# A gated trunk layer on one core: a written order for the products of neighbouring up pairs, row loads tied to the weights in the down stage, and the half sums of eight weight pairs made in the first half's output stage

## The chip, the cores and the metric

The kernel runs on one core of one Trainium2 chip. The metric is the device time of one execution in microseconds (us); lower is better. Engines are named as in the profile: PE is TensorE's matmuls, PEld its weight loads, DVE is VectorE, ACT is ScalarE, POOL is GpSimd, SP is SyncE, which here only issues transfers. "SPq", "POOLq" and "ACTq" are the transfer queues of the engines that issue them.

## What is computed

One layer, 1024 positions by 1024 channels, in float32: a layer norm, a wide projection, a convolution branch and a state space branch, their gated sum times w_o, a layer norm, a gated MLP with a causal convolution of three taps, a layer norm.

```
h = layer_norm(x)
u = h @ w_in                      # glu | z | x,B,C | dt | gate_a | gate_b
y_a = conformer(u_glu)            # causal convolution of 31 taps
y_b = ssd(z, xBC, dt)
h = layer_norm(a*h + (sigmoid(gate_a)*y_a + sigmoid(gate_b)*y_b) @ w_o)
up = causal_conv3(h @ w_ffn_up)   # 1024 -> 2 * 2816
gate, val = split(up)
h = layer_norm(a*h + (silu(gate) * val) @ w_ffn_down)
```

## The kernel before, in words

Every product of two matrices is made of three matmuls (`mm3`, L163): each operand is split into a rounded high part (ACT copies it into the type that PE takes, L154, L740) and the rest (DVE subtracts, L155, L741), and high*high, high*low and low*high are added in one PSUM bank. So each weight tile costs one load from HBM (SP), one cast on ACT and one subtraction on DVE before PE can use it. PSUM has two pools of four banks, `acc` and `sm`.

The positions are worked in two halves of 512. For each half come `ln_in`, `mixers` (four groups of columns, convolutions and the state space part) and `combine`. For the first half `out_proj` (L665) then multiplies by w_o in two passes q of 512 channels. A pass holds all four `acc` banks, one for each block of 128 positions; after it DVE adds the residual rows, `r = ALPHA*r + acc` (L687), which frees the banks for the next pass. The rows `r` (four tiles, pool `rows0`, L118) are loaded from `h_scr` by SP (L670). The four rows of x of the second half are normalised meanwhile by `ln_in(1)`, and `first_columns` (L348) of the second half's mixers follows on PE.

In the second half `ffn_blocks` works w_o and forms sums of blocks of the normalised rows, with which the up product (1024 x 1024 by 1024 x 5632) is made by seven products of half blocks in place of eight. A pair j of two weight tiles, with blocks a11, a12 | a21, a22, needs four half sums on DVE (L848 to L851) and the splits w24, w10 and w3; from pair 8 on also the split `ue` of the raw tile. LEAD = 8: for the first eight pairs two of the seven products (of raw tile 2j with b11 and b21) are made ahead by `up_first` (L815) while the last rows are still being normalised, and wait in HBM (`first_scr`). `up_rest` (L857) makes the other five products of a pair (of pairs 8 to 21 all seven), evicts the banks on the way (L868, L871, L878, L880, L883, L884, L886, L888), runs the three taps on DVE and ACT, gates, and stores. The sums of one bank go on after a copy was taken: PE may add to `ps` again only when ACT has read it.

`down` multiplies by w_ffn_down in seven products p of 11 steps k in the same way. Its residual rows (8 tiles of 1024 numbers, tile `rows`) are loaded by POOL in `load_rows` (L950), called at step 4 of the products 0, 1, 2 and 4.

What sets the order: the program is written in this sequence, and a scheduler (`schedule_with_timeline_sim`, L1237) reorders the instructions of each engine by data, buffers and priorities; `tc.high_priority(offset=n)` moves a block ahead. On the chip each engine then goes through its own list in order, and a waiting instruction holds all behind it, transfers included. Pools are memory regions stacked one above the other: a pool that opens after another has closed takes the same addresses, and its tiles wait for the last use of what lay there. `comb0`, `rows0`, `mixers1`, `trans` and `up` all begin at the same address.

```
with pool("rows0") as pl:
    rs = [pl.tile([P, D], F32, name=f"r0_{t}") for t in range(4)]
    out_proj(pl, rs, 0, mixT)
```

Of the kernel before, what the change touches and what calls it, by code (L numbers as in the profile page):

```python
# [16 lines left out]
P = 128  # L17
# [39 lines left out]
def kernel(  # L57
# [79 lines left out]
    h_scr = [dram.tile([HALF, D], F32, name=f"h_scr{i}") for i in range(2)]  # L137
    h1_scr = dram.tile([T, D], F32, name="h1_scr")
    first_scr = [dram.tile([2, P, HALF], F32, name=f"first_scr{j}") for j in range(LEAD)]
    NK = NF // 2  # L140
    b11_scr = [dram.tile([P, HALF], F32, name=f"b11_scr{k}") for k in range(NK)]
    b2_scr, t32_scr, t41_scr = (
# [669 lines left out]
            "t4": lambda i: b2[0][:, i, 4:8, :],  # L812
        }

    def up_first(upp, fp, bl, j):  # L815
# [12 lines left out]
        for q, block in enumerate(("b11", "b21")):  # L828
            product(ps, lambda i: w[i][:, q * HALF : (q + 1) * HALF], bl[block], q == 0)
            f = fp.tile([P, HALF], F32, tag="first", bufs=2, name=f"first{q}_{j}")  # L830
            A.copy(f, ps)
            A.dma_start(first_scr[j][1 - q], f)

    def up_weights(upp, j):


        with tc.high_priority(offset=2000):
            r1 = wst.tile([P, D], F32, tag="st", name=f"ra{j}")
            SY.dma_start(r1, wup[2 * j])
            if j:  # L840
                r2 = upp.tile([P, D], F32, tag="raw", bufs=3, name=f"rb{j}")
            else:
                r2 = wst.tile([P, D], F32, tag="st", name=f"rb{j}")
            SY.dma_start(r2, wup[2 * j + 1])
            a11, a12, a21, a22 = r1[:, :HALF], r1[:, HALF:], r2[:, :HALF], r2[:, HALF:]
            ue = None if j < LEAD else split_pair(wsp, r1, f"ue{j}")
            s3 = upp.tile([P, HALF], F32, tag="s3", name=f"s3_{j}")
            V.tensor_tensor(out=s3, in0=a11, in1=a21, op=ALU.add)  # L848
            V.tensor_tensor(out=a21, in0=a21, in1=a22, op=ALU.add)
            V.tensor_tensor(out=a11, in0=a21, in1=a11, op=ALU.add)  # L850
            V.tensor_tensor(out=a12, in0=a12, in1=a11, op=ALU.add)  # L851
# [5 lines left out]
    def up_rest(upp, us, bl, j, before, ws):  # L857

        ue, w24, w10, w3 = ws or up_weights(upp, j)
        ug, uv = us[2 * j % 3], us[(2 * j + 1) % 3]
        s = upp.tile([P, HALF], F32, tag="s", bufs=2, name=f"s{j}")
        early, late = slice(2, 2 + HALF), slice(2 + HALF, 2 + T)
        ps, pz = bank(1), bank(0)
        if ue:
            product(ps, lambda i: ue[:, i, :HALF], bl["b11"], True)
            A.copy(s, ps)  # L868
            py = bank(1)
            product(py, lambda i: ue[:, i, HALF:], bl["b21"], True)  # L870
            V.tensor_tensor(out=ug[:, early], in0=s, in1=py, op=ALU.add)  # L871
        else:
            with tc.high_priority(offset=2500):
                SY.dma_start(
                    ug[:, 2 : 2 + T].rearrange("p (q n) -> p q n", q=2),
                    first_scr[j].rearrange("q p n -> p q n"),
                )
            A.copy(ps, ug[:, late])  # L878
        product(ps, lambda i: w24[:, i, :HALF], bl["t2"], False)
        A.copy(s, ps)  # L880
        product(pz, lambda i: w3[:, i], bl["t3"], True)
        product(ps, lambda i: w10[:, i, :HALF], bl["t1"], False)
        A.copy(uv[:, late], ps)  # L883
        V.tensor_tensor(out=uv[:, late], in0=pz, in1=uv[:, late], op=ALU.subtract)  # L884
        product(pz, lambda i: w10[:, i, HALF:], bl["t4"], False)
        V.tensor_tensor(out=uv[:, early], in0=pz, in1=s, op=ALU.subtract)  # L886
        product(ps, lambda i: w24[:, i, HALF:], bl["b22"], False)
        A.copy(ug[:, late], ps)  # L888
        os = []
        j = j // 2 + j % 2 * NK  # L890
        for jj, u in ((j, ug), (NF + j, uv)):
# [25 lines left out]
        early, late = slice(0, HALF), slice(HALF, T)  # L917
        if j < NK:
            G.dma_start(b11_scr[j], ov[:, early])
            return ov  # L920
        SY.dma_start(b2_scr[j - NK], ov)
        a, b, t = before, ov, og
        V.tensor_tensor(out=t[:, early], in0=a[:, late], in1=b[:, late], op=ALU.subtract)
        V.tensor_tensor(out=a[:, late], in0=a[:, early], in1=a[:, late], op=ALU.subtract)
        V.tensor_tensor(out=t[:, late], in0=t[:, early], in1=a[:, early], op=ALU.subtract)
# [4 lines left out]
    def down(upp, dp):  # L930
# [16 lines left out]
        E, L = slice(0, HALF), slice(HALF, D)  # L947
        gb = []

        def load_rows(p):  # L950
# [140 lines left out]
        for p, (banks, first, then) in enumerate(products):  # L1091
            end = NK - LAST if p == 6 else NK
            for k in range(end):
                w = load(p, k)
                for t in range(4):
                    block(banks[t], w, t, first, k)
                if k == 4 and p in (0, 1, 2, 4):
                    load_rows(p)
# [35 lines left out]
    with pool("firsts", side="right") as fp:  # L1134
        for j in range(LEAD):
            if j == LEAD - 1:
                ws = up_weights(upp, 0)
            up_first(upp, fp, bl, j)
    before = None
    for j in range(NF):  # L1140
        before, ws = up_rest(upp, us, bl, j, before, ws), None
    ffn_stack.close()
    dp = ctx.enter_context(pool("down", side="right"))
    down(upp, dp)
# [99 lines left out]
```

## Time and profile before

| | us |
|---|---|
| median of 3 runs | 2024.91 |
| lowest and highest | 2024.34, 2026.39 |
| the profiled execution | 2030.47 |
| its span, first to last instruction | 2028.8 |
| PE busy | 1975.8 (97%) |
| DVE busy | 1695.8 (84%) |
| ACT busy | 1017.4 (50%) |
| POOL busy | 175.5 (9%) |

Times in the views count from the start of the span. Stages on PE in this execution: first half until 658, x's transposes and the second w_o pass to 686, `first_columns` 686 to 704, the second half's mixers from there, the up pairs from about 1400 to 1797, the down stage from there to the end. In a row of a group, the number behind "x" is the count, then come busy time in us, the mean in ns, and behind the second bar the idle time of the engine just before these instructions with what ended it. "PEclk" is the granted TensorE clock as a share of full speed.

### The profile page before, as it was taken

How to read it: one execution, taken by the hardware profiler on the slowest of the kernel's cores; microseconds unless marked ns; L12 is line 12 of the kernel's file. 1: busy time of each engine (PE TensorE's matmuls, PEld its weight loads, DVE VectorE, ACT ScalarE, POOL GpSimd, SP SyncE). 2: the span in 40 equal slices, each digit the busy share in tenths (PEclk: the TensorE clock that was granted, in tenths of full speed). 3: DMA queues.
4: the chain of work that ended last, by engine and by line, in shares of the span. 5: the costliest groups of instructions: out<-in, count | busy, mean ns of one | idle time of the engine just before them, and what ended most of it. 6: DMA issues, size and time to landing. Idle time of an engine off the chain costs nothing.

```text
span 2028.8 us, 24542 instructions
## 1 busy us (share of the span) xinstructions
PE 1975.8 (97%) x9164; PEld 1622.4 (80%) x9164; DVE 1695.8 (84%) x2261; ACT 1017.4 (50%) x1480; POOL 175.5 (9%) x140
## 2 busy tenths in 40 slices
PE   7999999999999999999999999999999999999998
PEld 6888888888788888888888888887777777777886
DVE  7599999989766869999998976596897777788768
ACT  4465654556453356665454645364554534443432
POOL 2010101001400000110100130010000000030000
PEclk9999999999999999999999999999999999999999
DMA  6222233333546522222323354565342222367563
GB/s 219 94 64 93 79 103 104 99 104 101 175 131 220 194 94 73 91 81 77 126 89 104 109 167 139 186 234 202 135 172 83 99 107 102 101 252 252 176 225 109
DMA packets 96903, 272.20 MB, mean 134 GB/s; under 512 B 11088, under 2 KB 11088, under 8 KB 96784
## 3 DMA queue, kind: packets, MB, share of 16 engines
q1 hardware_dynamic: 88864, 246.78, 36.8%
q0 software_dynamic: 5616, 19.66, 2.5%
q10 hardware_dynamic: 2304, 4.20, 0.6%
q8 instruction: 72, 1.18, 0.2%
q14 instruction: 47, 0.39, 0.1%
HBM read 221.05 MB, written 49.55 MB: 133 GB/s over the span
## 4 chain that ended last, share of the span: by engine, by line
PE 72%; DVE 19%; DMA 4%; issue 3%; ACT 2%; SPq 0%; DVEq 0%; ACTq 0%
PE acc L166 19%; PE acc L167 19%; PE acc L168 19%; DVE c L420 6%; PE sm L168 3%; PE sm L166 3%; PE sm L167 3%; PE sm L534 2%; PE acc L357 1%; DVE xbc L375 1%; DVE fo L898 1%; DMA dr<-b_scr 1%; PE sm L515 1%; PE sm L192 1%; PE sm L523 1%
## 5 line engine op out<-in xcount | busy, mean ns | idle before, releaser
L420 DVE SCALAR_TENSOR_TENSOR c<-v,pc,c 128x512 f32<-128x512 f32 x480 | 374.9, 804 | 6.3 <-ACT c L409 4.9
L478 POOL TENSOR_TENSOR au<-seg_mv,head_of 128x1024 fp32r<-128x1024 f32 x32 | 76.4, 2388 | 959.1 <-PE sm L487 728.8
L166 PE MATMUL acc<-hT,w_c 128*128 128x512 f32 x352 | 141.0, 401 | 0.0
L167 PE MATMUL acc<-hT,w_c 128*128 128x512 f32 x352 | 140.6, 399 | 0.0
L168 PE MATMUL acc<-hT,w_c 128*128 128x512 f32 x352 | 138.4, 393 | 0.0
L898 DVE SCALAR_TENSOR_TENSOR fo<-u,pc,fo 128x1024 f32<-128x1024 f32 x88 | 111.4, 1279 | 7.5 <-ACT fo L894 7.4
L375 DVE SCALAR_TENSOR_TENSOR xbc<-u,pc,xbc 128x512 f32<-128x512 f32 x144 | 109.9, 775 | 0.7 <-ACT xbc L373 0.5
L166 PE MATMUL acc<-h1s,w_s 128*128 128x512 f32 x264 | 103.6, 396 | 6.3 <-ACT s L880 3.7
L167 PE MATMUL acc<-h1s,w_s 128*128 128x512 f32 x264 | 102.9, 390 | 0.0
L168 PE MATMUL acc<-h1s,w_s 128*128 128x512 f32 x264 | 102.8, 391 | 0.0
L167 PE MATMUL acc<-w_z,hT 128*128 128x512 f32 x256 | 100.8, 394 | 0.0
L166 PE MATMUL acc<-w_z,hT 128*128 128x512 f32 x256 | 100.8, 401 | 0.0
L168 PE MATMUL acc<-w_z,hT 128*128 128x512 f32 x256 | 100.7, 396 | 0.0
L1032 ACT CAST w_dn<-dr 128x1024 fp32r<-128x1024 f32 (+1 forms) x73 | 60.9, 842 | 75.8 <-DVE dr L962 37.8
L154 ACT CAST w_c<-st_c 128x1024 fp32r<-128x1024 f32 x50 | 52.5, 1051 | 88.9 <-PE acc L168 68.2
L1033 DVE TENSOR_TENSOR w_dn<-dr,w_dn 128x1024 fp32r<-128x1024 f32 (+1 forms) x73 | 69.8, 963 | 15.3 <-ACT w_dn L1032 15.1
L167 PEld LDWEIGHTS acc<-hT,w_c 128*128 128x128 f32 x352 | 66.1, 188 | 16.9 <-issue 3.9
L168 PEld LDWEIGHTS acc<-hT,w_c 128*128 128x128 f32 x352 | 66.1, 188 | 16.2 <-issue 2.6
L166 PEld LDWEIGHTS acc<-hT,w_c 128*128 128x128 f32 x352 | 66.1, 188 | 15.9 <-issue 2.6
L166 PE MATMUL acc<-h1b,w_ue 128*128 128x512 f32 x168 | 67.3, 400 | 11.1 <-ACT w_ue L740 8.4
L155 DVE TENSOR_TENSOR w_c<-st_c,w_c 128x1024 fp32r<-128x1024 f32 x47 | 60.5, 1288 | 20.2 <-ACT w_c L154 20.2
L740 ACT CAST w_s<-rb 128x1024 fp32r<-128x1024 f32 x22 | 23.0, 1048 | 98.4 <-PE sm L168 63.8
(353 smaller groups left out, 5755.4 us busy)
## 6 DMA issues: line engine op xcount, KB each, us to landing
st_c<-wcol SPq DMA_DIRECT2D x50, 512.0 KB, 3.5
st_z<-wz SPq DMA_DIRECT2D x32, 512.0 KB, 3.5
st_wo<-wo SPq DMA_DIRECT2D x24, 512.0 KB, 4.0
ra<-wup SPq DMA_DIRECT2D x22, 512.0 KB, 3.6
rb<-wup SPq DMA_DIRECT2D x22, 512.0 KB, 3.4
t_scr<-fo POOLq DMA_DIRECT2D x22, 512.0 KB, 3.8
dr<-t_scr SPq DMA_DIRECT2D x44, 256.0 KB, 3.5
dr<-wdown SPq DMA_DIRECT2D x38, 256.0 KB, 3.9
```

Of the source, the lines that this page charges most:

```text
L154: A.copy(w[:, 0, :], st)
L155: (eng or V).tensor_tensor(out=w[:, 1, :], in0=st, in1=w[:, 0, :].bitcast(F32), op=ALU.subtract)
L166: TE.matmul(ps, wa(0), xa(0), start=start, stop=False, skip_group_check=more)
L167: TE.matmul(ps, wa(0), xa(1), start=False, stop=False, skip_group_check=more)
L168: TE.matmul(ps, wa(1), xa(0), start=False, stop=stop, skip_group_check=more)
L375: V.scalar_tensor_tensor(out=o, in0=u[:, k : k + HALF], scalar=pc[:, wc + k : wc + k + 1], in1=o, op0=ALU.mult, op1=ALU.add,)
L420: V.scalar_tensor_tensor(out=accs[i], in0=v[:, k : k + HALF], scalar=pc[:, wc + k : wc + k + 1], in1=accs[i], op0=ALU.mult, op1=ALU.add,)
L478: G.tensor_tensor(out=au, in0=seg_mv[:, c, :].unsqueeze(1).to_broadcast([P, 8, P]), in1=head_of[:, g, :].unsqueeze(2).to_broadcast([P, 8, P]),
L534: TE.matmul(py[:, hs], m[:, h, :], xs[:, hs], start=True, stop=True)
L898: V.scalar_tensor_tensor(out=o, in0=u[:, k : k + T], scalar=pc[:, wc + k : wc + k + 1], in1=o, op0=ALU.mult, op1=ALU.add,)
L1032: A.copy(w[:, 0, cs], src)
L1033: V.tensor_tensor(out=w[:, 1, cs], in0=src, in1=w[:, 0, cs].bitcast(F32), op=ALU.subtract)
```

## The change

Three edits are made together.

**Half sums made early.** `lead_sums` runs between `combine(0)` and `ln_in(1)`, in a pool `sums` of one buffer. For each of the eight leading pairs it loads both raw tiles (two transfers of 512 KB on POOL's queue), makes the four half sums on DVE, and stores the result, 128 x 2560 numbers or 1.25 MB, to `sums_scr` (POOL's queue). `up_weights` then loads the sums of these pairs in three pieces in place of the two raw tiles, and makes no sums for them. The pool lies at the address where `comb0` lay, on 10,240 bytes of each partition: exactly the six kilobytes of the tag "gate" (tiles `gb`, `gl`) and the four of the tag "yb". `rows0` opens after it at the same address, so the tiles r_0, r_1 and half of r_2 lie on `sums`.

**Written order of products.** `up_rest` becomes a generator `up_pair` with two stops, and PE's order in the pairs is the written one (`manual_schedule`): pair j's first part, then pair j-1's last part (products with b22 and t4), then pair j's middle part. `first_scr` is read in two transfers, into `s` and `ug`, and the tag "s" gets a third buffer, which `up_first` uses for its results too (the pool `firsts` is gone).

**Later row loads.** `load_rows` first copies four numbers of each partition of the step's split weights into the rows' place on POOL, so its transfers wait until that split is made.

```
+    def lead_sums(pl):
+        for j in range(LEAD):
+            r = pl.tile([P, 2 * D + HALF], F32, tag="sums", name=f"sums{j}")
+            for i in range(2):
+                G.dma_start(r[:, i * D : (i + 1) * D], wup[2 * j + i])
+            sums_of_pair(*(r[:, i * HALF : (i + 1) * HALF] for i in range(5)))
+            G.dma_start(sums_scr[j], r)
...
 mixT = combine(0, hT, yT)
+with pool("sums") as pl:
+    lead_sums(pl)
 hT = ln_in(1)
...
+            if j < LEAD:
+                ue = None
+                SY.dma_start(r1, sums_scr[j][:, :D])
+                SY.dma_start(s3, sums_scr[j][:, 2 * D :])
+                SY.dma_start(r2, sums_scr[j][:, D : 2 * D])
...
+    with tc.manual_schedule(engines={mybir.EngineType.PE}):
+        pairs = [up_pair(upp, us, bl, 0, kept, ws)]
+        next(pairs[0])
+        next(pairs[0])
+        for j in range(1, NF + 1):
+            if j < NF:
+                pairs.append(up_pair(upp, us, bl, j, kept, None))
+                next(pairs[j])
+            next(pairs[j - 1], None)
+            if j < NF:
+                next(pairs[j])
...
+            G.tensor_copy(
+                rows.rearrange("p (t n) -> p t n", n=D)[:, t0 : t0 + 4, cs.start : cs.start + 1],
+                w[:, 0, :4].bitcast(F32).unsqueeze(2),
+            )
```

How it moves instructions, at three places. Line numbers in the rows are those of the kernel that the row belongs to.

DVE in the first half's output stage, before: `r` are the residual rows that take up the w_o product (`acc`) and free its banks, `x` and `hT` belong to the normalisation of the second half.

```order
L227 SCALAR_TENSOR_TENSOR x_3_5153<-x_3_5153,mv_in_3_5234,in_g 128x1024
L223 RECIPROCAL rs_in_2_5210<-rs_in_2_5210 128x1
L687 SCALAR_TENSOR_TENSOR r_0_5263<-r_0_5263,acc_5279 128x512
L687 SCALAR_TENSOR_TENSOR r_1_5264<-r_1_5264,acc_5280 128x512
L687 SCALAR_TENSOR_TENSOR r_2_5265<-r_2_5265,acc_5281 128x512
L199 TENSOR_TENSOR hT_5143<-sm_5170,hT_5143 128x4x128
L223 RECIPROCAL rs_in_3_5235<-rs_in_3_5235 128x1
L199 TENSOR_TENSOR hT_5143<-sm_5177,hT_5143 128x4x128
L687 SCALAR_TENSOR_TENSOR r_3_5266<-r_3_5266,acc_5282 128x512
```

DVE at the same place now, the last sums and what follows them; the sums of pairs 1 to 7 (28 rows) stand in one piece ahead of `r_0`, and the sums of pair 0 among the steps on x.

```order
L826 TENSOR_TENSOR sums_5210<-sums_5210 128x512
L827 TENSOR_TENSOR sums_5210<-sums_5210 128x512
L828 TENSOR_TENSOR sums_5210<-sums_5210 128x512
L829 TENSOR_TENSOR sums_5210<-sums_5210 128x512
L688 SCALAR_TENSOR_TENSOR r_0_5339<-r_0_5339,acc_5355 128x512
L208 BN_STATS st_o_0_5351<-r_0_5339 128x6
L688 SCALAR_TENSOR_TENSOR r_1_5340<-r_1_5340,acc_5356 128x512
```

The four additions that read the banks of the first w_o pass have moved from behind the mean step of x_3 to behind the sums of all eight pairs.

SP's list around the loads of these rows, before:

```order
L203 DMA in_b<-prow 128x1024
L203 DMA ln_g<-prow 128x1024
L203 DMA ln_b<-prow 128x1024
L670 DMA r_0_5263<-h_scr_123 128x1024
L670 DMA r_1_5264<-h_scr_123 128x1024
L670 DMA r_2_5265<-h_scr_123 128x1024
L670 DMA r_3_5266<-h_scr_123 128x1024
```

And now:

```order
L258 DMA h_scr_124<-x_2_5227 128x1024
L258 DMA h_scr_124<-x_3_5229 128x1024
L204 DMA ln_g<-prow 128x1024
L204 DMA ln_b<-prow 128x1024
L671 DMA r_0_5339<-h_scr_123 128x1024
L671 DMA r_1_5340<-h_scr_123 128x1024
L671 DMA r_2_5341<-h_scr_123 128x1024
L671 DMA r_3_5342<-h_scr_123 128x1024
L153 DMA st_c_36_5654<-wcol 128x1024
```

The loads of the rows stand behind the stores of the normalised x, and in the program the first of them waits for all eight of POOL's transfer semaphores and for DVE's last sum; loads of the next stage's weights (`st_c_36` and on) are queued behind them.

PE among the up pairs 10 and 11, before (`w_ue_12414` is pair 11's raw tile, `w_s_10` are pair 10's sums; an `acc` is one bank):

```order
L167 MATMUL acc_12305<-h1s_10450,w_s_10_12295 128x512
L168 MATMUL acc_12305<-h1s_10450,w_s_10_12295 128x512
L166 MATMUL acc_12432<-h1b_10382,w_ue_12414 128x512
L167 MATMUL acc_12432<-h1b_10382,w_ue_12414 128x512
L166 MATMUL acc_12447<-h1b_10382,w_ue_12414 128x512
L167 MATMUL acc_12447<-h1b_10382,w_ue_12414 128x512
L168 MATMUL acc_12432<-h1b_10382,w_ue_12414 128x512
```

And now:

```order
L167 MATMUL acc_12453<-h1b_10458,w_ue_12436 128x512
L168 MATMUL acc_12453<-h1b_10458,w_ue_12436 128x512
L169 MATMUL acc_12453<-h1b_10458,w_ue_12436 128x512
L167 MATMUL acc_12320<-h1s_10524,w_s_10_12310 128x512
L168 MATMUL acc_12320<-h1s_10524,w_s_10_12310 128x512
L169 MATMUL acc_12320<-h1s_10524,w_s_10_12310 128x512
```

Pair 11's two raw products, which stood interleaved behind pair 10's product with t2, are now whole products, and pair 10's last two stand between them.

More of the change, by code (lines that the diff above doesn't have):

```diff
@@ L870, in up_rest @@
             product(py, lambda i: ue[:, i, HALF:], bl["b21"], True)
[L871 to L880, printed above, removed]
+            with tc.high_priority(offset=300):
+                V.tensor_tensor(out=ug[:, early], in0=s, in1=py, op=ALU.add)
@@ L881, in up_rest @@
+            t2()
         product(pz, lambda i: w3[:, i], bl["t3"], True)
         product(ps, lambda i: w10[:, i, :HALF], bl["t1"], False)
-        A.copy(uv[:, late], ps)
-        V.tensor_tensor(out=uv[:, late], in0=pz, in1=uv[:, late], op=ALU.subtract)
+        with tc.high_priority(offset=300):
+            A.copy(uv[:, late], ps)
+            V.tensor_tensor(out=uv[:, late], in0=pz, in1=uv[:, late], op=ALU.subtract)
+        yield
+        product(ps, lambda i: w24[:, i, HALF:], bl["b22"], False)
@@ L885, in up_rest @@
+        A.copy(ug[:, late], ps)
         product(pz, lambda i: w10[:, i, HALF:], bl["t4"], False)
         V.tensor_tensor(out=uv[:, early], in0=pz, in1=s, op=ALU.subtract)
-        product(ps, lambda i: w24[:, i, HALF:], bl["b22"], False)
-        A.copy(ug[:, late], ps)
         os = []
@@ L1133 @@
         G.memset(u[:, :2], 0.0)
[L1134 to L1141, printed above, removed]
+    for j in range(LEAD):
+        if j == LEAD - 1:
+            ws = up_weights(upp, 0)
+        up_first(upp, bl, j)
+    kept = []
+    with tc.manual_schedule(engines={mybir.EngineType.PE}):
[9 more added lines that the diff above has]
+                next(pairs[j])
     ffn_stack.close()
```

59 lines of the change are left out of this document (37 added, 22 removed).

## The prediction

> **What bounds the kernel now.** I read the page first, then PE by stage.
>
> ```profile
> PE 1975.8 (97%) x9164; PEld 1622.4 (80%) x9164; DVE 1695.8 (84%) x2261; ACT 1017.4 (50%) x1480; POOL 175.5 (9%) x140
> ```
>
> PE is the bound: only 53 of 2028.8 us are idle. So the change can win no more than PE's holes where it works, and whatever makes PE wait in a stage that has no holes is lost whole. The stages, in one answer (us, then busy us of each engine with its count, the granted clock, the share of the transfer engines and GB/s):
>
> ```profile
> core 0: us, PE busy (x) PEld busy (x) DVE busy (x) ACT busy (x) POOL busy (x), PEclk, DMA share, GB/s
> 638.00:662.00 24.00, 22.59 (x107) 18.52 (x106) 18.05 (x28) 7.76 (x13) 0.00 (x0) 1.00 0.91 350
> 662.00:704.00 42.00, 41.37 (x258) 37.41 (x259) 35.42 (x51) 10.87 (x17) 0.00 (x0) 1.00 0.49 176
> ...
> 1380.00:1400.00 20.00, 17.27 (x63) 13.48 (x62) 14.56 (x20) 10.40 (x17) 0.02 (x1) 0.83 0.89 306
> 1400.00:1500.00 100.00, 93.66 (x400) 74.10 (x399) 76.69 (x90) 46.85 (x60) 3.95 (x7) 1.00 0.38 133
> 1500.00:1600.00 100.00, 96.19 (x418) 77.67 (x416) 79.38 (x91) 46.41 (x59) 4.26 (x8) 1.00 0.31 111
> 1600.00:1700.00 100.00, 97.19 (x424) 79.03 (x423) 79.78 (x91) 47.73 (x58) 3.74 (x7) 1.00 0.28 98
> 1700.00:1800.00 100.00, 96.06 (x416) 77.05 (x415) 79.16 (x89) 45.75 (x55) 10.53 (x13) 1.00 0.35 124
> 1820.00:1840.00 20.00, 16.62 (x61) 13.17 (x60) 12.07 (x19) 7.32 (x15) 2.70 (x5) 0.83 0.89 307
> ```
>
> Two of the three edits aim at the lower six rows: in the pairs, 1400 to 1800, PE idles 400 - 383.1 = 16.9 us, and around 1390 and 1830 it idles 2.7 and 3.4 us, each time with the clock down to 0.83 over 20 us, another 3.4 us. The third edit works in the first two rows, where PE is busy for 64 of 66 us. PE's waits, by cause:
>
> ```profile
> PE acc L166 <- ACT w_ue L740: 8.4, 6, 1.4
> PE acc L166 <- ACT s L880: 3.7, 5, 0.9
> PE acc L166 <- ACT w_dn L1032: 3.4, 1, 3.4
> PE acc L166 <- ACT first L831: 2.7, 1, 2.7
> PE acc L166 <- ACT u L883: 2.7, 3, 1.7
> PE sm L166 <- ACT w_s L740: 2.0, 3, 1.3
> ```
>
> **The written order.** The copy that a bank waits for, and the cast and the subtraction of a weight tile, on ACT, ACT and DVE:
>
> ```profile
> L880 ACT COPY s<-acc 128x512 f32<-128x512 f32 x22 | 12.8, 580 | 5.6 <-PE acc L168 5.6
> ```
>
> ```profile
> L740 ACT CAST w_s<-ra 128x1024 fp32r<-128x1024 f32 x22 | 23.1, 1052 | 16.4 <-PE acc L168 12.7 <-PE sm L168 3.5
> ```
>
> ```profile
> L741 DVE TENSOR_TENSOR w_s<-ra,w_s 128x1024 fp32r<-128x1024 f32 x22 | 27.2, 1235 | 6.2 <-ACT w_s L740 6.2
> ```
>
> The waits on w_ue, s, u and w_s are those of the pairs: 8.4 + 3.7 + 2.7 + 2.0 = 16.8 us. The banks' copies (s, u) get at least one whole product of the neighbour pair, 12 matmuls of some 0.23 us (64 in 14 us, further down) or 2.7 us, between being written and being added to, and a copy takes 0.58 us; these waits should go. The wait on w_ue is for a weight buffer that PE has just left (three buffers, three tiles a pair). In the new order the tightest buffer is that of w24: freed by the b22 product, needed again two products or 5.4 us later, against a cast of 1.05 and a subtraction of 1.24 us on two engines in turn, on a DVE that is busy 79 of 100 us. It fits if neither stands behind much. I take 15 of the 16.8 us, bounds 5 and 18. The half sums that leave these pairs (8 x 4 additions) cost nothing here now and so win nothing by themselves; their loads grow from 1 to 1.25 MB a pair, hidden at a transfer share of 0.3 to 0.4.
>
> The hole at 1390 is PE waiting for a result's buffer, whose store takes long among other transfers; the one at 1830 is a weight operand that arrives late, in the same way:
>
> ```profile
> 1383.81 6.99 DMA first_scr<-first
> ```
>
> ```profile
> 1812.67 15.16 DMA dr<-b_scr
> ```
>
> A third buffer for the first covers 2.7 us more; the stage's transfers stay. I take 3 of its 2.7 + 3.4 us, bounds 0 and 6. **The later row loads** take 4 MB out of the start of the down stage, where dr lands after 15 us, and put 1 MB behind four splits, with six steps of 12 matmuls (16 us) before the rows are used: I take 6 of 3.4 + 3.4 us, bounds 0 and 7. Together the two edits win 24 us, bounds 5 and 31.
>
> **The sums made early.** Before, the chain here runs from combine's last gate tile (L660, L661) over x and r to PE's second w_o pass and on to the end of first_columns, where L166 comes back:
>
> ```profile
> 636.90 0.70 DVE gl L660
> ...
> 640.34 6.87 DMA x<-x
> 647.22 10.91 DMA r<-h_scr
> ...
> 661.90 0.60 DVE r L687
> 662.63 0.47 PE acc L166
> ...
> 686.50 17.27 PE acc L357 x144
> 703.77 0.23 PE acc L166
> ```
>
> The buffer `sums` lies on combine's gate tiles, so the first load can start only when L661 has read the last of them:
>
> ```profile
> 637.62 0.69 DVE L661 TENSOR_TENSOR mb<-mb,gl 128x512 f32<-128x512 f32 x1
> ```
>
> That is 638.3. Eight rounds follow in the one buffer, each of which must end before the next starts: two loads, four additions, one store. After the last, r_0 can be loaded (it lies on `sums`), then DVE can free a bank, then PE can start the second pass. Nothing else on PE can go ahead: in its list everything stands behind that pass, but for x's transposes. DVE stands in the sums as well, with r_0 behind them. The prices:
>
> ```profile
> L849 DVE TENSOR_TENSOR rb<-rb 128x512 f32<-128x512 f32 x22 | 15.1, 685 | 0.1
> ```
>
> ```profile
> rb<-wup SPq DMA_DIRECT2D x22, 512.0 KB, 3.4
> t_scr<-fo POOLq DMA_DIRECT2D x22, 512.0 KB, 3.8
> b_scr<-fo POOLq DMA_DIRECT2D x11, 256.0 KB, 2.3
> ```
>
> ```profile
> L927 POOL DMA_DIRECT2D t_scr<-fo x11 | 5.9, 534 | 195.4 <-issue 127.7 <-DVE fo L925 51.0 <-ACT w_s L740 16.6
> ```
>
> ```profile
> 642.00:656.00 14.00, 14.00 (x64) 11.58 (x63) 10.00 (x18) 4.93 (x6) 0.00 (x0) 1.00 1.02 394
> 656.00:662.00 6.00, 4.59 (x28) 3.63 (x26) 6.00 (x8) 2.22 (x6) 0.00 (x0) 1.00 1.03 412
> ```
>
> With all transfer engines busy they move some 403 GB/s, so 512 KB more take 1.3 us more. Loads: the second is issued 0.53 us after the first and lands after 3.4, plus the 0.77 us by which the first's bytes are still ahead of it: 4.7. Additions: 4 x 0.685 = 2.7. Store of 1.25 MB: from the 512 KB row 3.8 + 1.95 = 5.75, from the 256 KB row 2.3 + 2.6 = 4.9; the middle, 5.3. Hand-overs between engines: 0.2, an estimate. A round: 12.9 us. Low end, no byte costs beyond the 512 KB rows: 0.53 + 3.4 + 2.7 + 3.8 + 0.2 = 10.6. High end, bytes strictly one after the other at the rows' prices: 7.2 + 2.7 + 2.5 x 3.8 + 0.2 = 19.6. I take 12.9, nearest to what overlapping transfers give.
>
> The Trainium skill, page "DMA: Bandwidth & Descriptors", section "Anatomy of one DMA — SWDGE (gpsimd) path", fits a transfer from GpSimd's queue as about 2.0 us and its bytes at 436 GB/s; an estimate from that is 4.4 for the loads, 5.0 for the store, 12.3 a round and 4 us less in all. The t_scr row agrees within a fifth: 3.2 by the fit, 3.8 in the row.
>
> Round 0 runs among the loads and the steps on x: its last addition stands ahead of x_3's mean step, which began at 660.55 in the chain before, with three sums ahead of it; so it ends at about 660.5 + 4 x 0.685 = 663.3, and its store at 668.6.
>
> ```profile
> 660.55 1.27 DVE x L227
> ```
>
> Seven rounds: 668.6 + 7 x 12.9 = 758.9. Load of r_0 3.5 (rb's row, rounded up), addition 0.7, hand-over 0.2: PE restarts at 763.3 in place of 662.6. From there before took 703.8 - 662.6 = 41.2 us to the end of first_columns, of which the transposes of x_2 and x_3 (1.8) are then done: 763.3 + 39.4 = 802.7, or 98.9 later. The mixers behind it are PE bound (9 in every slice of the page's row), so nothing is won back there. And PE restarts after 90 idle us: by the two rows with the clock at 0.83, an idle stretch of about 3 us costs 3.4 us more in clock. I add 3: 102. With the low round 86, with the high one 149.
>
> ```profile
> PE   7999999999999999999999999999999999999998
> ```
>
> The Trainium skill, page "TensorE: Matmul & The Clock Gate", Part 1, says that one idle window of about 3.4 us halves the clock until about as long a busy window has passed; that makes 1.7 us after the stall, and the sum 1 us less. The trace agrees on the halving, but holds it twice as long (20 us x 0.17 x 2 = 6.8 us) and starts it after 2.7 idle us.
>
> **The sum.** 2024.9 + 102 - 24 = 2103. Against the profiled execution itself, 2030.5, which lies 5.6 above the median, the same sum is 2108.5.
>
> **The rivals.**
>
> *Dearer rounds.* Loads and stores from POOL's queue don't overlap, or are slower alone than these rows: 16 us a round give 2103 + 7 x 3.1 = 2125, the high end 2103 + 47 = 2150. For it: t_scr's spread in the trace; against it: at that time nothing else is on the queues. 14 in 100.
>
> *No gain in the pairs.* The new order puts PE's waits on weights in place of those on banks: DVE, in the pairs busy 79 of 100 us, must deliver w24 within 5.4 us. It decides where cast, subtraction and what stands ahead of them on DVE take longer than that, three steps of 1.3 us. Then 2103 + 15 to 24 = 2118 to 2127. 20 in 100.
>
> *Faster: the sums are hidden.* If the eight rounds were over before PE needs the banks, the stage would lose nothing and the kernel would come to 2025 - 24 = 2001. The point from which this decides is an end of the rounds by about 659, from 638: 2.6 us a round, less than the additions alone. Even overlapped, 18.9 MB at 403 GB/s take 47 us, 26 too many, which eats the 24. It needs that the order or the buffers are not what I read. 4 in 100, with equality 1 of them.
>
> *The forecast*, rounds near 12.9 and most of the two gains: 62 in 100, 2085 to 2118.
>
> **The range.** Low: rounds of 10.6 with the full gain of 31: 2025 + 86 - 31 = 2080; I put 2078 for the first round's place. High: rounds of 17 with the gain of 24, 2025 + 131 - 24 = 2132, which also takes in the case without gain. Outside lie the dearest rounds and the hidden sums, some 12 in 100. A measurement of this kernel can tell about 0.2%, 4 us, from no change; faster by more than that 0.03, within 0.01, slower 0.96.
>
> **What would show it.** In the profile after: PE idle in one piece of about 90 to 100 us between 670 and 765, ended by DVE's r_0; eight store issues on POOL 12 to 14 us apart; DVE almost idle there; the clock low just after. In the pairs, PE waits of under 5 us in all, the waits on s and u gone. At 1830 before (about 1925 then) no hole, and rows' transfers in four groups. The prediction is wrong if PE's second w_o pass starts before 740 or after 800, or if the pairs show the same 17 us of waits.

## The result and the profile after

The changed kernel takes 2142.3 us (median of 4 runs, 2140.6 to 2143.1), the kernel before 2025.7 us beside it (4 runs, 2024.3 to 2028.8): a ratio of 1.0571, 95% interval 1.0555 to 1.0587. It is 117 us slower, where 78 were forecast, and lies 10 us above the range.

The page of the changed kernel begins with these rows of busy time and of the span in slices:

```profile
PE 1977.2 (92%) x9164; PEld 1628.9 (76%) x9164; DVE 1697.7 (79%) x2261; ACT 1023.6 (48%) x1480; POOL 188.9 (9%) x168
...
PE   7999999999994059999999999996899999999998
...
PEclk9999999999996579999999999998999999999999
```

PE has as many busy us as before (1977.2 against 1975.8) in a longer span. It idles in two places: the large hole, in slices 13 to 15, and a smaller one in slices 28 and 29, where the first products of the leading pairs are made. PE's waits by cause name both:

```profile
PE acc L167 <- DVE r L688: 97.3, 1, 97.3
PE sm L193 <- DVE x L231: 23.6, 4, 12.5
PE acc L167 <- ACT first L847: 15.3, 4, 10.8
PE sm L759 <- DVE r L231: 7.1, 1, 7.1
PE acc L167 <- ACT acc L895: 2.6, 1, 2.6
```

The first row is the stall that was forecast. The wait for x was 14.8 us in the kernel before; of the growth, 8.3 us lie between 630 and 720 (9.5 against 1.2), just ahead of the stall. The waits on s, u and w_s of the kernel before are gone. The wait for the copy `first` has grown from 2.7 to 15.3 us, and 7.1 us for a normalised row and 2.6 us for `acc` are new.

**The large hole.** The chain of waits through it, with the first two rounds and the end:

```profile
666.58 5.13 DMA sums_scr<-sums
671.71 0.28 issue
671.99 0.53 POOL sums L821
672.52 7.41 DMA sums<-wup
...
680.05 0.70 DVE sums L826
680.78 0.70 DVE sums L827
681.50 0.70 DVE sums L828
682.23 0.70 DVE sums L829
682.93 0.28 issue
683.21 4.71 DMA sums_scr<-sums
...
688.21 0.52 POOL sums L821
688.73 4.83 DMA sums<-wup
...
764.19 4.73 DMA sums_scr<-sums
...
769.06 3.36 DMA r<-h_scr
...
772.55 0.70 DVE r L688
773.38 0.77 PE acc L167
```

Store, load, four additions, store, without a gap, and only behind the last store the row r_0: the mechanism is the one the prediction described. From the landing of round 0's store (671.71) to that of the last (764.19 + 4.73 = 768.92) seven rounds take 97.2 us, 13.9 each; the later ones take 13.3 to 13.7.

**The pairs.** The windows of the up pairs, with the columns of the prediction's rows from 1400 to 1800:

```profile
1530.00:1550.00 20.00, 15.20 (x52) 11.45 (x53) 1.56 (x2) 5.62 (x10) 0.00 (x0) 0.83 0.48 157
1550.00:1650.00 100.00, 100.00 (x440) 82.21 (x439) 81.23 (x87) 57.23 (x71) 4.88 (x9) 1.00 0.51 166
1650.00:1750.00 100.00, 100.00 (x440) 82.40 (x439) 83.54 (x98) 49.05 (x58) 4.84 (x9) 1.00 0.29 102
1750.00:1850.00 100.00, 100.00 (x440) 82.40 (x439) 80.10 (x92) 51.06 (x60) 3.77 (x7) 1.00 0.29 103
```

From 1550 on PE does not wait at all. The first row is the end of the leading products, with PE idle for almost 5 of 20 us.

**The leading products.** ACT's timeline in the changed kernel, around the first of the 16 copies that free their banks:

```profile
1489.88 0.62 ACT L764 CAST h1s<-ts 128x512 fp32r<-128x512 f32 x1 [0.34 <-DVE ts L792]
1493.01 0.62 ACT L764 CAST h1b<-ts 128x512 fp32r<-128x512 f32 x1 [2.51 <-DVE ts L795]
1493.53 0.58 ACT L847 COPY first<-acc 128x512 f32<-128x512 f32 x1
```

And in the kernel before:

```profile
1352.87 0.62 ACT L763 CAST h1b<-ts 128x512 fp32r<-128x512 f32 x1
1353.39 0.57 ACT L831 COPY first<-acc 128x512 f32<-128x512 f32 x1
1354.35 0.59 ACT L763 CAST h1s<-sm 128x512 fp32r<-128x512 f32 x1 [0.39 <-DVE ts L789]
```

Before, the copy stood among the casts of the last normalised rows, 3.0 us after the leading products had begun on PE (1350.34). Now it stands behind the very last cast, 31.8 us after that beginning (1461.76). Until then PE can't add to the banks that it has filled, and it stops. The addresses in the built program say why: the tag "s", where `first` now lies, takes 135,520 to 141,664 bytes of a partition, and the three buffers of the last normalised rows (tag "row" of the pool `trans`) take 131,040 to 143,328. The old pool `firsts` lay at 176,096, beyond the end of `trans` at 170,208. The last use of those rows ends sooner than the copy begins: PE's last transposes of them at 1483.3, the store of the last row by about 1487. The copy follows the cast ahead of it without a pause, so the last 6.5 us are its place in ACT's list, behind all the casts.

### The profile page after: what moved, and what is told of

It is laid out like the page before. It is cut to its first block, busy times and chain, and to the rows that moved or that the text cites. A ratio compares the mean times of both kernels' runs of the same rounds, so it can differ in the third digit from the quotient of the medians.

```text
span 2141.4 us, 24665 instructions
## 1 busy us (share of the span) xinstructions
PE 1977.2 (92%) x9164; PEld 1628.9 (76%) x9164; DVE 1697.7 (79%) x2261; ACT 1023.6 (48%) x1480; POOL 188.9 (9%) x168
## 4 chain that ended last, share of the span: by engine, by line
PE 71%; DVE 19%; DMA 6%; issue 3%; ACT 1%; POOL 0%; SPq 0%; DVEq 0%; POOLq 0%; ACTq 0%
PE acc L167 18%; PE acc L169 18%; PE acc L168 18%; DVE c L421 6%; PE sm L168 3%; PE sm L167 3%; PE sm L169 3%; DMA sums_scr<-sums 2%; DMA sums<-wup 2%; PE sm L535 1%; PE acc L358 1%; DVE xbc L376 1%; PE sm L516 1%; PE sm L524 1%; DVE w_c L156 1%
## 5 line engine op out<-in xcount | busy, mean ns | idle before, releaser
L167 PE MATMUL acc<-w_wo,mixT 128*128 128x512 f32 x128 | 48.7, 399 | 99.2 <-DVE r L688 97.3
L167 PEld LDWEIGHTS acc<-w_wo,mixT 128*128 128x128 f32 x128 | 24.5, 192 | 105.5 <-issue 97.6
L155 ACT CAST w_wo<-st_wo 128x1024 fp32r<-128x1024 f32 x24 | 25.3, 1055 | 154.7 <-PE acc L169 145.8
L1064 DVE TENSOR_TENSOR w_dn<-dr,w_dn 128x1024 fp32r<-128x1024 f32 (+1 forms) x73 | 70.3, 969 | 13.9 <-ACT w_dn L1063 13.6
L168 PEld LDWEIGHTS acc<-hT,w_c 128*128 128x128 f32 x352 | 66.1, 188 | 16.9 <-issue 3.8
L169 PEld LDWEIGHTS acc<-hT,w_c 128*128 128x128 f32 x352 | 66.1, 188 | 16.1 <-issue 2.6
```

What stands on the lines that cost most here:

```text
L155: A.copy(w[:, 0, :], st)
L167: TE.matmul(ps, wa(0), xa(0), start=start, stop=False, skip_group_check=more)
L168: TE.matmul(ps, wa(0), xa(1), start=False, stop=False, skip_group_check=more)
L169: TE.matmul(ps, wa(1), xa(0), start=False, stop=stop, skip_group_check=more)
L1064: V.tensor_tensor(out=w[:, 1, cs], in0=src, in1=w[:, 0, cs].bitcast(F32), op=ALU.subtract)
```

## The experiments

Sums by place, from PE's timeline in the profiled run of each kernel. Up to the second half's w_o product the change loses 110.7 us (1299.60 before, 1410.31 after), and from there to the first leading product 0.7. The up stage, from the first leading product to the last product of a pair, takes 7.2 more (454.7 before, 461.9 after), and the down stage behind it 6.5 less (214.2 and 207.7). The experiments take these terms apart, and this table has the two stages of each kernel as well, with the part of the up stage in which PE is idle:

| kernel | up stage, us | PE idle in it, us | down stage, us |
|---|---|---|---|
| before | 454.7 | 19.6 | 214.2 |
| the change | 461.9 | 27.9 | 207.7 |
| e1 | 465.1 | 30.4 | 208.0 |
| e2 | 428.3 | 1.4 | 207.8 |
| e3, e11 | 435.6, 436.6 | 6.8, 7.5 | 207.8, 207.8 |
| e5 | 430.3 | 3.0 | 207.7 |
| e9 | 428.5 | 1.4 | 207.8 |
| e10 | 439.6 | 10.3 | 207.8 |
| e12 | 434.9 | 5.8 | 211.6 |
| e13 | 452.8 | 18.6 | 207.8 |

The times, and what the labels stand for:

| kernel | median, us | ratio to before, 95% interval |
|---|---|---|
| the change | 2142.3 | 1.0571, 1.0555 to 1.0587 |
| without early sums (e1) | 2034.4 | 1.0037, 1.0024 to 1.0051 |
| first results in their old pool (e2) | 2107.9 | 1.0397, 1.0381 to 1.0412 |
| both of these (e3) | 2007.5 | 0.9904, 0.9887 to 0.9920 |
| e2, sums' buffer at another place (e4) | 2064.9 | 1.0185, 1.0169 to 1.0200 |
| e2, four early sums (e5) | 2060.0 | 1.0154, 1.0139 to 1.0169 |
| e2, two buffers for the sums (e6) | 2077.3 | 1.0241, 1.0226 to 1.0256 |
| e3, row loads as before (e7) | 2009.0 | 0.9903, 0.9887 to 0.9920 |
| e4, additions on POOL (e9) | 2013.6 | 0.9919, 0.9899 to 0.9939 |
| e1, tag s at another place (e10) | 2010.4 | 0.9907, 0.9893 to 0.9920 |
| e3 again (e11) | 2006.2 | 0.9887, 0.9873 to 0.9900 |
| e7 again (e12) | 2009.2 | 0.9904, 0.9890 to 0.9917 |
| later row loads alone (e13) | 2022.0 | 0.9964, 0.9951 to 0.9978 |

**e1: no early sums.**

```
-    with pool("sums") as pl:
-        lead_sums(pl)
...
-            if j < LEAD:
-                ue = None
-                SY.dma_start(r1, sums_scr[j][:, :D])
-                SY.dma_start(s3, sums_scr[j][:, 2 * D :])
-                SY.dma_start(r2, sums_scr[j][:, D : 2 * D])
-            else:
...
+            ue = None if j < LEAD else split_pair(wsp, r1, f"ue{j}")
```

> The changed kernel without the early half sums: all 22 pairs load their raw tiles and make their sums where they are used, as in the kernel before; written order, later row loads and the buffers of the first products stay as changed. Theory (the 111 us stall is the chain of eight rounds; the leading products lose some 27 us because their result tiles now lie where the last normalised rows lie): the stall goes, the loss in the leading products stays, 2142 - 111 = 2031 us. Rival (the leading products lose because the sums' 1.25 MB loads and the changed DVE order of the leading pairs come late): both go, 2142 - 111 - 27 = 2004 us.

Measured: 2034.4 us; the theory said 2031, the rival 2004. PE's waits in this kernel:

```profile
PE acc L167 <- ACT first L847: 15.3, 4, 10.8
PE sm L193 <- DVE x L231: 15.2, 3, 12.6
PE sm L759 <- DVE r L231: 7.1, 1, 7.1
```

The 97 us are gone, and the waits of the leading products are the same to the tenth. So they have nothing to do with the sums or their loads.

**e2: the first results in their old pool.**

```
-            f = upp.tile([P, HALF], F32, tag="s", bufs=3, name=f"first{q}_{j}")
+            f = fp.tile([P, HALF], F32, tag="first", bufs=2, name=f"first{q}_{j}")
...
-        s = upp.tile([P, HALF], F32, tag="s", bufs=3, name=f"s{j}")
+        s = upp.tile([P, HALF], F32, tag="s", bufs=2, name=f"s{j}")
...
+    with pool("firsts", side="right") as fp:
```

> The changed kernel with the pool of two result buffers for the first products put back at its old place, outside the rows' addresses (the tag s of the pairs goes back to two buffers to make room). Theory (place of the result tiles): the leading products get back what they lost, 2142 - 27 = 2115 us, stall unchanged at 97 us in one piece. Rival (loads of the sums are the cause): 2142 us, and a hole of 20 us on PE near 1480 as before. Rival two (the third buffer of s is what frees the pairs): the gain of 27 is partly given back in the pairs, 2120 to 2130.

Measured: 2107.9 us, 34 under the change where 27 were expected. PE's longest wait is the stall as it was, and next to it only the wait for x is large, of which 10.3 us fall between 630 and 720, just ahead of the stall (1.6 in e3, which makes no early sums):

```profile
PE acc L167 <- DVE r L688: 97.6, 1, 97.6
PE sm L193 <- DVE x L231: 22.9, 5, 12.2
```

Of the second rival, nothing shows: two buffers of s are enough for the pairs.

**e3: both.** The edits of e1 and e2 together; what is left of the change is the written order and the later row loads.

> The changed kernel without the early half sums and with the old pool of result buffers: written order and later row loads alone. Theory: 2142 - 111 - 27 = 2004 us, bounds 1997 and 2010, that is about 21 under the kernel before, 15 to 20 of it in the pairs and about 6 at the start of the down stage. Rival (the pairs' gain comes from the early sums, which take 22 us of additions off DVE there): 2015 to 2022.

Measured: 2007.5 us, 0.9904 of before, faster than both kernels. e1 and e3 differ by the place of the first results alone (and the third buffer of s): 26.9 us by the medians, and in the up stage 29.5 (465.1 and 435.6), of which 23.6 are idle time of PE. e2 and e3 differ by the early sums alone: 100.4 us, made of 108.0 us lost by the second half's w_o product (1301.17 on PE in e3, 1409.18 in e2) and 7.3 won back in the up stage (435.6 and 428.3), 5.4 of them idle time of PE.

**e10: the same three buffers of s at another place.** e1 with one difference, to part the place from the number of buffers and from the sharing of a tag:

```
     upp = ctx.enter_context(pool("up"))
+    sp = ctx.enter_context(pool("s"))
...
-            f = upp.tile([P, HALF], F32, tag="s", bufs=3, name=f"first{q}_{j}")
+            f = sp.tile([P, HALF], F32, tag="s", bufs=3, name=f"first{q}_{j}")
```

> The changed kernel without the early half sums (2034.4 us), and with one difference: the tag s, three buffers shared by the first products' results and the pairs' copies as in the change, lies in a pool of its own above the pool up, behind the last byte of the normalised rows' pool. No pool of result buffers. Theory (the place alone makes the loss of 27 us in the leading products): 2034.4 - 27 = 2007 us, or up to 3 less, since three buffers cover the 3 us for which PE waits on the results with two. Rival (sharing the three buffers between the first results and the pairs' copies is what holds up the leading products): 2030 or more.

Measured: 2010.4 us, 24 under e1. The tag now begins at 170,464, behind the last byte of `trans`. ACT makes the first copy as early as in the kernel before, by its timeline:

```profile
1353.46 0.58 ACT L847 COPY first<-acc 128x512 f32<-128x512 f32 x1
```

So the address is the cause; with it moved, the copy comes right behind the same cast as before. (With the tag gone from the pool `up`, other tiles there, `rb` and `s3` among them, move down by its 6 KB too, to where e3 has them; that this small move does nothing by itself was not tested.) The third buffer gives nothing over two: e11, measured beside it, takes 2006.2 us, with an up stage 3.0 us shorter. PE waits 3.2 us for `first` in e10 and 3.1 in e11, and 4.8 against 2.2 for `acc`, into which ACT copies `s` when its load has landed.

**e5: half the dose.**

```
+    EARLY_SUMS = 4
...
-        for j in range(LEAD):
+        for j in range(EARLY_SUMS):
...
-            if j < LEAD:
+            if j < EARLY_SUMS:
...
-                ue = split_pair(wsp, r1, f"ue{j}")
+                ue = None if j < LEAD else split_pair(wsp, r1, f"ue{j}")
```

> As the kernel with the early sums and the old pool of result buffers (2107.9 us), but half sums made early for four of the eight leading pairs; the other four are made where they are used. Theory (a chain of rounds in one buffer, 13.5 us each): four rounds fewer, 2107.9 - 4 x 13.5 = 2054 us, with PE's hole at 97.6 - 54 = 44 us. Rival (a fixed price for the pool standing between combine and the output stage): the hole shrinks by much less than half, over 2075.

Measured: 2060.0 us. PE's wait for r_0 shrinks from 97.6 to 43.2 us, by the row of its waits:

```profile
PE acc L167 <- DVE r L688: 43.2, 1, 43.2
```

That is 54.4 for four rounds, 13.6 each. The price of this wait goes with the number of rounds, and no fixed one shows. The kernel as a whole gains less, 47.9 us by the medians, which is why it misses the 2054 of the theory by 6: the up stage is 2.0 us longer than in e2, with four pairs that make their sums there again, and the profiled run takes 4 us longer between PE's restart and the first leading product, which was not taken apart.

**e6: two buffers for the sums.**

```
-            r = pl.tile([P, 2 * D + HALF], F32, tag="sums", name=f"sums{j}")
+            r = pl.tile([P, 2 * D + HALF], F32, tag="sums", bufs=2, name=f"sums{j}")
```

> As the kernel with the early sums and the old pool of result buffers (2107.9 us), but two buffers for the sums, at the same place under the output stage's rows. Theory (each round waits for the one before because there is one buffer): the loads of one round run beside additions and store of the other, 13.5 / 2 = 6.8 us a round at best, 5.9 us if only the 2.25 MB at 403 GB/s count; seven rounds 47 us shorter, 2061 us, bounds 2050 and 2075. Rival (loads and stores of POOL's queue go one after the other whatever the buffers): no shorter than 9.5 us a round, 2080 or more.

Measured: 2077.3 us, 30.6 under e2, between the two forecasts. The chain of waits in its last rounds:

```profile
703.37 6.57 DMA sums<-wup
...
709.97 3.15 issue
...
713.12 4.75 DMA sums_scr<-sums
...
718.16 0.53 POOL sums L821
718.68 6.55 DMA sums<-wup
```

Here each buffer has a chain of its own, and the loads of both run side by side: 6.6 us (4.5 to 4.8 with one buffer), 3.2 for what stands as "issue" between them and the store (the four additions), 4.8 for the store, 0.8 to the next load, 15.3 in all, in which two rounds are done. That is 7.7 a round where half of 13.5 was expected, since the loads take 2 us longer beside other transfers. The rival's 9.5 us a round did not come. PE's wait for r_0 is 62.4 us, 35 less than in e2, where 47 less were expected.

**e4: one buffer, at another place.** e2, with the pool `sums` opened above 26,624 bytes that nothing uses:

```
-    with pool("sums") as pl:
-        lead_sums(pl)
+    with pool("below") as pl:
+        pl.tile([P, 6656], F32, name="below")
+        with pool("sums") as pl2:
+            lead_sums(pl2)
```

> The changed kernel with the old pool of result buffers, and the early half sums kept whole, but their one buffer 26 KB higher, where neither the output stage's rows nor combine's gate tiles lie; the mixers use that place only in their second column group. Eight rounds, 18.9 MB and 32 additions stay. Theory (the stall is the wait of the residual rows for the buffer's place): PE restarts its second pass near 663, and the kernel takes 2004 to 2016. Rival (bytes and additions cost what they cost, wherever the buffer lies): 47 us of transfers at 403 GB/s beside a DVE that is busy 84% cost 20 to 47, so 2024 to 2051. A third way: the additions, in DVE's list in order, wait for late loads and hold up what stands behind them: over 2051.

Measured: 2064.9 us, the third way. The wait for r_0 is gone: the second w_o pass begins at 665.62 (662.63 in the kernel before), so the address was what held it. But PE stops again, some 50 us later, and its waits name one cause:

```profile
PE acc L167 <- ACT w_z L155: 56.9, 1, 56.9
```

DVE's longest wait on the sums (total, times, longest):

```profile
DVE sums L826 <- DMA sums<-wup: 51.2, 5, 10.6
```

And ACT's timeline where the hole ends, with the idle time before the instruction in brackets:

```profile
780.77 0.31 ACT L283 ACTIVATE sp<-sp 128x128 f32<-128x128 f32 x1 [62.67 <-DVE sp L282]
```

The rounds in the one buffer go on until 780: the first three stores are issued 28 and 17 us apart, the last four 13.4 to 13.5. Their additions stand in DVE's list ahead of `sp` (the time steps of the mixers), DVE waits 51.2 us for their loads, ACT waits 62.7 us for `sp`, and the casts of w_z stand behind that on ACT. The first chain was removed and the same rounds came back through a list in order.

**e9: the additions on POOL.** e4 with one difference:

```
-            sums_of_pair(*(r[:, i * HALF : (i + 1) * HALF] for i in range(5)))
+            sums_of_pair(*(r[:, i * HALF : (i + 1) * HALF] for i in range(5)), G)
```

> As the kernel with the sums' buffer 26 KB higher (2064.9 us), but the 32 additions run on POOL in place of DVE. There the stall of 57 us remained, although the residual rows were free. Theory (what was left of the stall is DVE's list in order: additions that wait for late loads hold up the splits behind them): POOL has nothing else to do at that time, the rounds take some 5 + 4 x 1.6 + 5 = 16.5 us each, 132 in all, and end before POOL's next work at 742; 2007 to 2020 us, no hole over 5 us on PE between 660 and 800. Rival (bandwidth or the traffic of the sums is what costs): over 2030, with the hole still there.

Measured: 2013.6 us. The hole is gone, with all 18.9 MB and all 32 additions still there; so neither bytes nor additions as such made it, but who waits behind them. The rounds also lie earlier: POOL makes its first addition at 584, where DVE comes to it at 656 in e4. They take 21.6 us each where 16.5 were expected, and four of the eight stores are issued after 660, the last at 741.5, while PE goes on. PE's largest new wait is 4.2 us:

```profile
PE acc L167 <- ACT xbc L374: 4.2, 1, 4.2
```

Yet this is no faster than e3 (0.9919, 0.9899 to 0.9939, against 0.9904 and 0.9887), which makes no early sums: by the second half's w_o product it has lost 13.4 us (1314.57 against 1301.17 on PE), and it wins 7.1 back in the up stage (428.5 us against 435.6). Part of the loss is DVE's: two of its groups between 575 and 750 in e9,

```profile
L376 DVE SCALAR_TENSOR_TENSOR xbc<-u,pc,xbc 128x512 f32<-128x512 f32 x18 | 18.1, 1030 | 0.3 <-ACT xbc L374 0.2
L156 DVE TENSOR_TENSOR w_wo<-st_wo,w_wo 128x1024 fp32r<-128x1024 f32 x8 | 11.2, 1405 | 0.0
```

and the same two in e3:

```profile
L376 DVE SCALAR_TENSOR_TENSOR xbc<-u,pc,xbc 128x512 f32<-128x512 f32 x18 | 13.0, 742 | 0.6 <-ACT xbc L374 0.5
L156 DVE TENSOR_TENSOR w_wo<-st_wo,w_wo 128x1024 fp32r<-128x1024 f32 x8 | 9.6, 1204 | 0.0
```

Beside POOL's additions the same DVE step takes 1030 in place of 742 ns, and 1405 in place of 1204. A step with one of its two inputs in PSUM, `gl<-gl,acc`, stays at 688 ns (687 in e3) in the same stretch. The Trainium skill, page "SBUF — State Buffer", section "Who interferes with whom", says that a VectorE instruction with two inputs in SBUF contends with a GpSimd instruction that reads SBUF. These rows agree.

**e7, e12 and e13: the row loads.** e7 is e3 without the copy in `load_rows`, e12 the same kernel again beside e3 (e11), and e13 is the kernel before with that copy as the only edit:

```
+            G.tensor_copy(
+                rows.rearrange("p (t n) -> p t n", n=D)[:, t0 : t0 + 4, cs.start : cs.start + 1],
+                w[:, 0, :4].bitcast(F32).unsqueeze(2),
+            )
             for t in range(t0, t0 + 4):
                 G.dma_start(rs[t][:, cs], h1_scr[t * P : (t + 1) * P, cs])
```

> As the kernel with written order and later row loads alone (2007.5 us), but without the copy that ties the rows' loads to the weights: they are issued as in the kernel before. Theory (the term of 6 us for the hole at the start of the down stage): 2013.5 us, with a PE hole of about 3 us and the lower clock back at the start of the down stage. Rival (the down stage gains nothing from it, the whole gain of 20 is the written order): 2007.5 us.

> The kernel with written order and later row loads, with the old pool of result buffers, measured again beside the next two: 2007.5 us by the first measurement; it should stay within 3 us of that.

> The same without the later row loads, measured again with more rounds. The profile of the first measurement has a hole and lower clock of 3.4 us at the start of the down stage that the kernel with later row loads doesn't have. Theory: about 3 us slower than that, half of the 6 us of the prediction. Rival: no difference.

> The kernel before with the later row loads as the only edit. Theory (the term of the prediction: 3.4 us of hole and 3.4 us of clock at 1830 are the rows' transfers in the way): 2025 - 6 = 2019 us. Rival (the hole there comes from the order of the pairs, which hands the down stage its stored products late): within 3 us of the kernel before, and the hole is still there.

Measured: e13 takes 0.9964 of before (0.9951 to 0.9978), 7.3 us less: alone, the later row loads win what was forecast. On top of the written order the times tell less: e7 is level with e3 (2009.0 and 2007.5, overlapping), and e12 is 2.9 us above e11, with intervals that overlap too. The window at the start of the down stage parts them better than the times. In e12:

```profile
1805.00:1825.00 20.00, 18.05 (x73) 14.26 (x72) 15.45 (x26) 10.34 (x19) 2.17 (x4) 0.91 0.90 328
```

In e11, with the later row loads:

```profile
1805.00:1825.00 20.00, 20.00 (x90) 16.57 (x89) 15.80 (x26) 9.00 (x16) 4.70 (x9) 1.00 0.88 306
```

And in e13, where this place lies 15 us later:

```profile
1820.00:1840.00 20.00, 20.00 (x90) 16.54 (x90) 15.35 (x25) 8.00 (x14) 4.53 (x9) 1.00 0.92 306
```

With early row loads and the written order (e12) there are 2.0 us of hole and 1.8 of clock at that place, against 3.4 and 3.4 in the kernel before; with the later row loads both are zero, with either order. The down stage as a whole says the same: 214.2 us before, 211.6 in e12, 207.7 to 208.0 in every kernel of the table with the later loads. The two edits share one gain of 6.4, of which the order alone gets 2.6.

## Why the prediction was wrong, point by point

**The stall: right in mechanism, 9 us too small.** It said 102 us by one buffer, eight rounds and r_0 behind them. On PE it is 110.7 by the second half's w_o product between before and after, 108.0 between e3 and e2. e1, e5 and e4 show its three parts: no sums, no stall; half the rounds, half the wait; another address, no wait for r_0. The restart was put at 763.3 and came at 773.4. Of these 10.1 us, 3.1 are round 0 (its store landed at 671.7, not 668.6) and 6.9 the seven rounds (97.2 us, not 90.3). A steady round: two issues and the loads 5.1 to 5.4 (put at 4.7), additions 2.9 (2.7), store 4.7 (5.3), hand-overs 0.7 (0.2). Round 1 alone took nearly 3 us more, with its loads among the other transfers. After the restart the rest of the stage took 41.1 us, 1.3 less than the 42.4 it was given with its 3 us of clock. That term was read a little too high: the clock in the hole at 1390 fell 1.9 us after PE's last matmul, and 0.8 of its 6.8 us at half clock lay in the hole itself.

**The leading products: the step that failed.** The prediction said of the hole at 1390: "A third buffer for the first covers 2.7 us more; the stage's transfers stay. I take 3 of its 2.7 + 3.4 us, bounds 0 and 6." In its place stands a loss: 26.9 us by e1 against e3, 34.4 by the medians of the change and e2. The edit did not only add a buffer, it moved the results to another address, and there they wait for the last use of the normalised rows. e10 shows that it is the address: same tag, same three buffers, another place, 24 us less. The prediction used just this rule for `sums` on the gate tiles, and did not ask it of the second tile that changed its pool. The third buffer would not have won the 3 us at the old price either: in e10 PE's wait for `first` is as long as with two. Without this step, the sum was close: e2, the change with the old pool, is at 1.0397 of before, which on 2024.9 is 2105 us, against 2103 forecast. That it comes so close is partly luck: in e2 the stall is some 8 us dearer than forecast (109.6 by the second half's w_o product) and the up stage wins 8 us more (26.4 and not 18), and the two cancel.

**The written order: right, and a little larger.** It was put at 15 us. e12 (the order with the old pool, rows loaded as before) is at 0.9904 of before, some 19 us less, and its up stage is 19.9 us shorter than before. The forecast for this stage was 18, with the 3 us of the third buffer, which e10 shows to be worth nothing. The waits on banks' copies are gone, as said, and the weights keep up: PE is busy 100 of 100 us in three windows. The prediction counted waits alone; of the 19.9 us, 13.8 are idle time of PE (19.6 and 5.8) and 6.1 its busy time in the same 1875 matmuls (435.1 and 429.0), a term that it did not have. The edit also gives the copies a higher priority, exchanges the last two products of a pair and reads `first_scr` in two transfers; no run parts these from the written order.

**The later row loads: right.** The down stage wins 6.4 to 6.5 us where 6 were forecast, the two PE terms of the hole in the right place. Alone they give 7.3 us by the times.

**The half sums "win nothing by themselves": wrong by some 7 us.** Between e3 and e2 the up stage shrinks from 435.6 to 428.3 us, in e9 to 428.5. PE is idle there for 6.8 us in e3 and 1.4 in e2: its wait for `first` goes from 3.8 to 0.2 us and that for `acc` from 2.2 to 1.0. This is the hole at 1390 that the third buffer was to cover. It is a gain, but no version here kept it: e9 lost more before the up stage than it won there.

**The rivals.** "Dearer rounds" came a third of its way: 13.9 in place of 12.9, not 16. "No gain in the pairs" did not come. "The sums are hidden" is what e9 does, with another engine and another place, and it gives 2013.6, not 2001.

What stays open: by what path the early sums shorten PE's waits for `first` and `acc`, and why they win 7.3 us in the up stage with the old pool of first results and 3.2 without it (465.1 in e1, 461.9 in the change); and how the 13.4 us of e9 before the second half's w_o product divide between DVE's slower steps and the transfers.

## What to carry to other kernels

When an edit puts a tile into another pool or tag, look up what lay at its new address and when that is last used; do it for every tile that moved, also where the edit seems to add a buffer. A chain that uses one buffer costs its full round, times its rounds, to whatever comes next at that address, and to whatever stands behind it in an engine's list: taking away the first alone (e4) gave back 43 of 100 us, both (e9) 94. Work taken off an engine that isn't the bound can win little more than what the bound still waits for: in e3 PE is idle for 6.8 us of the up stage, and taking 32 additions off DVE there won 7.3.

## What the runs showed of the hardware

After the stall the clock came back sooner than after the two holes of the kernel before. The window behind PE's restart at 773.4:

```profile
773.00:780.00 7.00, 6.62 (x21) 5.41 (x22) 4.88 (x8) 0.00 (x0) 0.00 (x0) 0.70 0.38 152
```

A clock of 0.70 over 7 us is 4.2 us at half clock, 3.9 of them behind the restart, against the 6.8 that the prediction read from the rows before; the loss is 1.9 us where it took 3. The Trainium skill, page "TensorE: Matmul & The Clock Gate", Part 1, gives a busy window of about 3.4 us; this row is the nearer to it.

The length of the stop doesn't decide it. Read in finer windows, the granted clock is at 0.50 for stretches of 3.4 us or a multiple of it: 3.4 after PE's holes of 3.1 us in e3 and 2.0 us in e12, 6.8 after those of 2.7 and 3.4 us in the kernel before and of 4.8 us in e10, and 116.0 (34 times 3.41) over the whole stall, from 661.2 to 777.25. In e3 and e12 PE was at work again when the clock fell; in the three holes with 6.8 us it was not, and came back 0.8 to 1.9 us later. A hole of 2.4 us in e7 lies between: PE came back 0.5 us after the fall, and the clock after 3.4.

A store of 1.25 MB from POOL's queue landed 4.7 us after its issue, less than either value that the prediction worked out by rate from the 512 and 256 KB rows, 5.75 and 4.9.
